# Full-height stationary operands and one address residue for the operand pools of a hybrid attention block

## The chip, the cores and the metric

The kernel runs on one core of one Trainium2 chip. The metric is the device time of one execution in microseconds (us); the time of a version is the median of its runs.

## The reference

One decoder layer on x of 1024 tokens by 1024 features, all in fp32. With h = RMSNorm(x), one projection h @ W_in gives the inputs of three token mixers and their gates:

```
y_A = differential attention, 4 heads: softmax(q0 k0) - lam * softmax(q1 k1), times v of width 128
y_B = sliding window (128) attention with sinks, 8 query heads on 2 kv heads
y_C = compressed + selected + window (512) attention, 8 query heads on 2 kv heads, gated sum of three
x  <- x + W_o( sum_n sigmoid(G_n) * (y_n @ P_n) )
x  <- x + W_down relu(W_up RMSNorm(x))^2
```

A relative position bias is added to the token logits. For the compressed branch, keys and values of 32-token blocks are pressed through a small MLP, which leaves 63 positions (64 with padding) for each of the two kv heads.

## The kernel before, in words

**Products.** Each fp32 product is made of three matmuls (`mm3`, L115 to L120): every operand is split into a high and a low part in the fp32r format (`split`, L87: ScalarE writes the high part, VectorE or GpSimd the low part), and high x high (L118), high x low (L119) and low x high (L120) are summed in PSUM. In the trace a matmul is written `out<-moving,stationary`.

**Stages, in order of time.** (1) Norm and transposition of x (`norm_transpose`), the projection of the first head of A, the bias vectors and the compression MLP; (2) mixer A, head by head, to about 416 us; (3) mixer B; (4) mixer C, for each of its two kv heads a projection (`project_c`) followed by the attention items (`items_c`), from about 572 to 1210 us; (5) the branch products, W_o and the MLP. The MLP's two products use a seven-product (Strassen) form: 16 pairs x 7 products x 12 matmuls of 512 columns each way.

**Order.** TensorE's instructions run in the order in which the program emits them. `mix` (L155) interleaves the attention's steps ("fine") with pieces of dense work (the next projection, or the sigmoid gates of `gates`) by fixed estimates of TensorE and VectorE time. The instructions of the other engines, and the DMA queue of SyncE, are ordered by a planner that simulates the program.

**Mixer A's keys.** `project_a` projects q, k, v of a head, and `vec` writes a tile `tm` for each 128 tokens: q high/low of both components (256 columns), k high twice for each component (L588, 256 columns), k low of both components (L590, 128 columns). `to_state` transposes `tm` in groups of up to four blocks of 128 columns into one PSUM tile `tr` (L552) and copies the group into the state `st` (L556 on ScalarE, L558 on VectorE). The five blocks make a group of four and a group of one. In a logits row (`logits`, L702) there are two matmuls for each of the two components: the first has all 128 rows (q high and q low against k high, written twice), the second 64 rows (q high against k low); `n["logits"]` (L576, L577) holds the slices. For each head, tokens 0 to 511 make 2 such rows for each 128 tokens and tokens 512 to 1023 make 4: 24 a head, 96 in all.

**Mixer C's compressed values.** `compressed` (L1085) writes probabilities `pc` of 128 queries x 64 positions; `tp_c` transposes two of them (64 rows of output), and `pv_c` multiplies with `vct`, the compressed values as 64 rows x 128 columns (high and low side by side): two matmuls (L895, L896) for each of 32 items.

**Where tiles lie.** Pools are stacked from the left and from the right end of each partition's memory; a pool's address is the sum of the sizes before it. The addresses modulo 512 bytes, as the program of before lays them out:

| operand | stage | residue |
|---|---|---|
| `hh`, `hl` (normed x, transposed) | 1 to 4 | 480 |
| state `st` / weight forms `wh`, `wl` | mixers A, B | 320 / 320 + 64 k, k = 0 to 7 |
| state `st`, weight forms `wh`, `wl`, `xh`, `xl` | mixer C | 192 |
| probabilities `ph`, `pl` | mixers A, B / C | 160 / 480 |
| `mh`, `ml` (merged x), `t2` to `t4`, half of the branch weights, second half of `oc` | stage 5 | 416 |
| `ob`, first half of `oc`, `wo`, the other weight forms | stage 5 | 480 |
| `ident`, `identr` | all | 384, 416 |

**Bias vectors.** `bias_vectors(p0)` (L244) loads `rb`, `oh`, `mk`, multiplies (L378), adds into `bv` (L379) and stores to memory. It is emitted behind the first projection, with its tiles in the pool `p0` beside the tiles of x and the gain `g`.

## Time and profile before

| what | us |
|---|---|
| median of 3 runs | 2076.6 (2073.64 to 2076.71) |
| the profiled execution | 2073.64, its span 2073.6 |
| TensorE matmuls busy | 1950.6 (94%) |
| weight loads busy | 1615.6 (78%) |
| VectorE, ScalarE, GpSimd busy | 1420.5, 1019.3, 948.4 |

The span of the profiled execution is its device time to a tenth of a microsecond; nothing lies around it. Matmuls are pipelined: a row's duration is longer than what the matmul costs. The cost is the step from the start of one matmul to the start of the next, and most of the readings below are such steps. PEld is the engine's weight load, which can run while the matmul before it still streams. "issue" as the end of an idle time means that the engine waited for nothing that the profile shows.

### The profile page before, as it was taken

How to read it: one execution, taken by the hardware profiler on the slowest of the kernel's cores; microseconds unless marked ns; L12 is line 12 of the kernel's file. 1: busy time of each engine (PE TensorE's matmuls, PEld its weight loads, DVE VectorE, ACT ScalarE, POOL GpSimd, SP SyncE). 2: the span in 40 equal slices, each digit the busy share in tenths (PEclk: the TensorE clock that was granted, in tenths of full speed). 3: DMA queues.
4: the chain of work that ended last, by engine and by line, in shares of the span. 5: the costliest groups of instructions: out<-in, count | busy, mean ns of one | idle time of the engine just before them, and what ended most of it. 6: DMA issues, size and time to landing. Idle time of an engine off the chain costs nothing. (4 is left out here: it accounts for less than half of the span.)

```text
span 2073.6 us, 30616 instructions
## 1 busy us (share of the span) xinstructions
PE 1950.6 (94%) x9806; PEld 1615.6 (78%) x9806; DVE 1420.5 (69%) x3231; ACT 1019.3 (49%) x2626; POOL 948.4 (46%) x1137
## 2 busy tenths in 40 slices
PE   7999998998899999999999899999899998999998
PEld 7777777788688788787888677787688886888876
DVE  6757677788838767648676745657755444889898
ACT  5456555566636555536555533325445544434331
POOL 4555345354252212152221327217444444789784
PEclk9999999999999999999999899999999999999998
DMA  6131012011201111202142556425544346345343
GB/s 216 50 102 52 3 55 58 14 50 37 85 24 64 54 53 50 71 30 93 61 151 64 168 180 208 153 89 159 173 163 155 138 143 249 121 158 168 122 142 112
DMA packets 122557, 219.47 MB, mean 106 GB/s; under 512 B 14420, under 2 KB 35412, under 8 KB 122396
## 3 DMA queue, kind: packets, MB, share of 16 engines
q1 hardware_dynamic: 120812, 211.75, 31.3%
q10 hardware_dynamic: 1584, 5.77, 0.8%
q8 instruction: 77, 1.26, 0.3%
q14 instruction: 84, 0.69, 0.1%
HBM read 156.59 MB, written 64.81 MB: 107 GB/s over the span
## 5 line engine op out<-in xcount | busy, mean ns | idle before, releaser
L91 POOL TENSOR_TENSOR wl<-wr,wh 128x512 fp32r<-128x512 f32 (+3 forms) x246 | 326.1, 1332 | 282.1 <-ACT wh L90 236.8
L90 ACT ACTIVATE wh<-wr 128x512 fp32r<-128x512 f32 (+3 forms) x258 | 150.4, 591 | 182.3 <-PE mm L119 122.5
L705 PE MATMUL sc<-st 128*128 128x256 f32 (+5 forms) x736 | 201.6, 356 | 15.4 <-ACT p L737 15.0
L90 ACT ACTIVATE ph<-tr 128x384 fp32r<-128x384 f32 (+3 forms) x280 | 138.3, 496 | 118.0 <-PE tr L753 97.1
L91 DVE TENSOR_TENSOR pl<-tr,ph 128x384 fp32r<-128x384 f32 (+3 forms) x280 | 155.3, 558 | 45.7 <-ACT ph L90 42.4
L750 POOL MEMSET ph<- 128x128 f32 x152 | 34.7, 228 | 301.2 <-PE ac L895 256.6
L705 PEld LDWEIGHTS sc<-st 128*128 128x128 f32 x736 | 126.3, 192 | 55.7 <-ACT p L737 23.4
L118 PE MATMUL mm<-hh,wh 128*128 128x512 f32 x384 | 160.0, 417 | 0.0
L120 PE MATMUL mm<-hh,wl 128*128 128x512 f32 x384 | 152.5, 397 | 0.0
L119 PE MATMUL mm<-hl,wh 128*128 128x512 f32 x384 | 152.4, 397 | 0.0
L119 PE MATMUL mm<-wl,wh 128*128 128x512 f32 x352 | 140.4, 399 | 9.4 <-POOL wl L91 9.4
L118 PE MATMUL mm<-wh 128*128 128x512 f32 x352 | 140.5, 399 | 8.3 <-DVE x L1464 5.4
L753 PE MATMUL tr<-ident,p 128*128 128x128 f32 x792 | 132.3, 280 | 15.4 <-ACT o L883 7.9
L90 ACT ACTIVATE wh<-u 128x512 fp32r<-128x512 f32 x162 | 93.1, 620 | 107.8 <-PE mm L119 28.0
L120 PE MATMUL mm<-wh,wl 128*128 128x512 f32 x352 | 139.7, 397 | 0.0
L737 ACT ACTIVATE p<-sc,mc 128x256 f32<-128x256 f32 (+5 forms) x200 | 106.8, 538 | 51.0 <-DVE mc L729 48.9
L895 PE MATMUL ac<-ph,st 128*128 128x256 f32 x392 | 111.4, 302 | 17.2 <-DVE ob L902 11.3
L91 POOL TENSOR_TENSOR wl<-s,wh 128x512 fp32r<-128x512 f32 x64 | 87.8, 1379 | 82.8 <-ACT wh L90 82.8
L118 PE MATMUL mm<-wh,hh 128*128 128x384 f32 (+1 forms) x320 | 124.6, 389 | 0.0
L91 DVE TENSOR_TENSOR wl<-u,wh 128x512 fp32r<-128x512 f32 x98 | 110.4, 1128 | 4.1 <-ACT wh L90 4.1
L896 PE MATMUL ac<-pl,st 128*128 128x256 f32 x392 | 106.6, 293 | 5.8 <-DVE pl L91 5.2
L753 PEld LDWEIGHTS tr<-ident,p 128*128 128x128 f32 x792 | 92.0, 142 | 24.8 <-ACT o L883 10.5
(309 smaller groups left out, 5759.6 us busy)
## 6 DMA issues: line engine op xcount, KB each, us to landing
ud<-u SPq DMA_DIRECT2D x112, 256.0 KB, 2.1
u<-ud SPq DMA_DIRECT2D x98, 256.0 KB, 3.3
wr<-wu SPq DMA_DIRECT2D x76, 256.0 KB, 2.8
wr<-wd SPq DMA_DIRECT2D x64, 256.0 KB, 2.9
gd<-go SPq DMA_DIRECT2D x48, 256.0 KB, 2.0
g<-gd SPq DMA_DIRECT2D x48, 256.0 KB, 3.1
wr<-wg SPq DMA_DIRECT2D x40, 256.0 KB, 2.6
wr<-wbr SPq DMA_DIRECT2D x40, 256.0 KB, 3.0
```

What stands on the lines that cost most here:

```text
L90: nc.scalar.activation(hi, src, AF.Copy)
L91: (eng or nc.vector).tensor_tensor(lo, src, hi.bitcast(F32), op=ALU.subtract)
L118: mm(out, lh, rh, start=first, stop=False, skip_group_check=more)
L119: mm(out, lh, rl, start=False, stop=False, skip_group_check=more)
L120: mm(out, ll, rh, start=False, stop=last, skip_group_check=more)
L705: self.nc.tensor.matmul(ps[:, off:off + k1 - k0], q[:, t * P:(t + 1) * P], k[:, k0:k1], start=i == 0, stop=i == 1)
L737: self.nc.scalar.activation(p, ps, AF.Exp, bias=m, scale=-1.0, accum_out=l)
L750: nc.gpsimd.memset(ph[0:rows, o:o + P].bitcast(F32), 0.0)
L753: nc.tensor.transpose(pt[0:rows, o:o + P], src, self.ident)
L895: nc.tensor.matmul(ac, v, ph, start=first, stop=False)
L896: nc.tensor.matmul(ac, v, pl, start=False, stop=last)
```

## The change

The key's low part is written twice like its high part, so `tm` gets six blocks, the state grows from 7 x 1024 to 8 x 1024 columns, and the second logits matmul has 128 rows: (q high, q low) against (k low, k low). The compressed values get 64 zero rows, and the four `pc` tiles become fixed tiles of 128 columns whose upper half is zero, taken in turn. Spacer tiles of 96, 480 and 224 bytes move the left pools. By the sums of the sizes, the left pools of mixer C and of stage 5 and `ident`, `identr`, `kct`, `vct` come to residue 480, the states of A and B to 96 and their weight forms to 96 + 64 k. The bias vectors' tiles move from `p0` to the next pool `cp`, which takes `p0`'s place, and their sum is written in place.

```
-        self.st_n, self.tm_n = 7 * S, 768
+        self.st_n, self.tm_n = 8 * S, 768
...
-            self.bias_vectors(p0)
         with tc.tile_pool(name="cp", side="right", **kw) as cp:
+            self.bias_vectors(cp)
...
+        self.pcs = [self.at.tile([P, P], F32, name=f"pc{i}") for i in range(4)]
+        for x in self.pcs:
+            nc.gpsimd.memset(x[:, 64:P], 0.0)
...
     def idents(self):
+        self.cst.tile([P, 24], F32, name="gap0")
         self.ident = self.cst.tile([P, P], F32, name="ident")
...
         nc.vector.memset(self.nhalf, -0.5)
+        self.cst.tile([P, 120], F32, name="gap1")
...
+        c.tile([P, 56], F32, name="gap2")
         self.kct = c.tile([P, 2, P], F32R, name="kct")
-        self.vct = c.tile([64, 2, P], F32R, name="vct")
+        self.vct = c.tile([P, 2, P], F32R, name="vct")
+        nc.gpsimd.memset(self.vct[64:P].bitcast(F32), 0.0)
...
-        bv = pool.tile([20, 2, 384], F32, name="bv")
...
-            nc.vector.tensor_tensor(bv[:, i, :], ps[0:20, 0:384], mk[:, i, :], op=ALU.add)
+            nc.vector.tensor_tensor(mk[:, i, :], ps[0:20, 0:384], mk[:, i, :], op=ALU.add)
...
-                self.split(self.vct[:, :, 0:64], self.vct[:, :, 64:128], vr)
+                self.split(self.vct[0:64, :, 0:64], self.vct[0:64, :, 64:128], vr)
...
-        n = dict(st=st, v=st[:, 5 * S:7 * S].rearrange("p (t x e) -> p t x e", x=2, e=P), logits=[])
+        n = dict(st=st, v=st[:, 6 * S:8 * S].rearrange("p (t x e) -> p t x e", x=2, e=P), logits=[])
         for c in range(2):
-            half = slice(64 * c, 64 * c + 64)
-            n["logits"].append([(st[:, c * S:c * S + S], st[:, (2 + c) * S:(3 + c) * S]),
-                                (st[half, c * S:c * S + S], st[half, 4 * S:5 * S])])
+            q = st[:, c * S:c * S + S]
+            n["logits"].append([(q, st[:, (2 + c + x) * S:(3 + c + x) * S]) for x in (0, 2)])
...
-            kl = tm[:, 512:640].rearrange("p (c d) -> p c d", d=HD)
-            nc.vector.tensor_tensor(kl, y[:, 2:4, :], kd[:, :, 0, :].bitcast(F32), op=ALU.subtract)
+            kl = tm[:, 512:768].rearrange("p (c x d) -> p c x d", x=2, d=HD)
+            nc.vector.tensor_tensor(kl, y[:, 2:4, :].unsqueeze(2).to_broadcast([P, 2, 2, HD]), kd.bitcast(F32),
+                                    op=ALU.subtract)
...
-        return self.project(self.a["wa"][h], 384, vec, (st, [i * S for i in range(5)])), n
+        return self.project(self.a["wa"][h], 384, vec, (st, [i * S for i in range(6)])), n
...
-                    return hv(self.vct[:, g, :], ph[0:64, 0:256], pl[0:64, 0:256], True, False)
+                    return hv(self.vct[:, g, :], ph[:, 0:256], pl[:, 0:256], True, False)
...
-        p = mem["c"] = self.at.tile([P, 64], F32, name="pc", tag="pc", bufs=4)
+        p = mem["c"] = self.pcs[0]
+        self.pcs.append(self.pcs.pop(0))
...
-        self.expo(p, ps, m[:, 0, 0:1], l[:, 0, 0:1])
+        self.expo(p[:, 0:64], ps, m[:, 0, 0:1], l[:, 0, 0:1])
```

## The prediction

> **What bounds the kernel now.** I read, in this order, the page's head, the busy time by stretches, the waits, and then the order of time, where the step from one matmul's start to the next is what counts. First the stretches (columns: us, then busy us and count for each engine):

> ```profile
> span 2073.6 us, 30616 instructions
> ...
> 130.00:416.00 286.00, 267.41 (x1460) 216.65 (x1459) 202.99 (x586) 157.12 (x524) 126.78 (x193) 1.00 0.13 38
> 624.00:884.00 260.00, 250.44 (x1428) 211.43 (x1427) 184.99 (x604) 150.29 (x427) 55.37 (x113) 1.00 0.18 57
> 1508.00:1560.00 52.00, 52.00 (x225) 41.89 (x224) 26.42 (x36) 26.05 (x43) 24.22 (x19) 1.00 0.44 152
> 1768.00:1820.00 52.00, 52.00 (x231) 43.05 (x230) 44.55 (x57) 22.34 (x41) 40.04 (x27) 1.00 0.42 135
> ```

> TensorE is the bound in each: 94% in mixer A (130 to 416), 96% in C's first items, all of the time in the MLP's up product (1508) and down product (1768). VectorE, the next, has 71% in A and in C. So what counts is how long TensorE takes over its fixed list, and who would stop it if it went faster. Its waits in A, and one from C, say what it stops for now (us in all, times, longest):

> ```profile
> PEld sc L705 <- issue: 21.0, 85, 0.3
> PEld mm L118 <- issue: 13.7, 62, 0.2
> PEld tr L753 <- ACT o L883: 7.7, 8, 1.1
> PEld tr L753 <- DVE pl L91: 5.2, 5, 1.3
> ...
> PE ac L895 <- DVE ob L902: 4.2, 5, 1.0
> ```

> The two largest are waits for nobody: 34.7 us of "issue" before weight loads. They sit around the 64-row loads:

> ```profile
> 137.66 0.71 PE L705 MATMUL sc<-st 128*128 128x384 f32 x2
> 137.93 0.18 PEld L705 LDWEIGHTS sc<-st 64*128 64x128 f32 x1 [0.25 <-issue]
> 138.30 0.19 PEld L118 LDWEIGHTS mm<-wh,hh 128*128 128x128 f32 x1 [0.19 <-issue]
> 138.30 0.44 PE L118 MATMUL mm<-wh,hh 128*128 128x384 f32 x1
> 138.41 0.19 PEld L119 LDWEIGHTS mm<-wl,hh 128*128 128x128 f32 x1
> 138.58 0.34 PE L119 MATMUL mm<-wl,hh 128*128 128x384 f32 x1
> 138.76 0.34 PE L120 MATMUL mm<-wh,hl 128*128 128x384 f32 x1
> ```

> A full-height load begins while the matmul before it streams (138.41 beneath the one of 138.30). The 64-row load starts only at 137.93, and the full load behind it at 138.30, together with its own matmul. Three matmuls of 384 columns take 138.58 - 137.66 = 0.92 us, where the undisturbed step is 138.76 - 138.58 = 0.18: 0.38 us lost for each logits row.

> **The change part by part.** The sum is made against the profiled execution, 2073.6 us, which is 3.0 below the median of 2076.6.

> *The key's low part in 128 rows.* There are 96 such rows, so TensorE's list shrinks by 96 x 0.38 = 36.5 us (the 34.7 of "issue" is the same thing seen by the loads). The second matmul streams as many columns as before, so I give it the first one's step. Added in each of the 32 token blocks: one more transposition, a ScalarE copy of 256 columns instead of 128 (L556) and a low part of 256 columns instead of 128 (L590):

> ```profile
> L556 ACT ACTIVATE st<-tr 128x128 fp32r<-128x128 f32 x24 | 6.4, 266 | 6.5 <-PE tr L552 6.5
> L556 ACT ACTIVATE st<-tr 128x256 fp32r<-128x256 f32 x4 | 1.5, 381 | 2.7 <-PE tr L552 2.7
> L590 DVE TENSOR_TENSOR tm<-y,tm 128x128 fp32r<-128x128 f32 x24 | 8.7, 362 | 1.5 <-ACT tm L588 1.1
> ```

> The copy grows by 0.115 us (3.7 in all, ScalarE); the low part I let grow as much (3.7, VectorE). A transposition costs TensorE no more than the (794.54 - 794.13) / 4 = 0.10 us of the rows below: 3.3 us in all. The list is then 33 us shorter. How much arrives? VectorE's share of A would rise from 203 / 286 = 71% to 207 / 253 = 82%, and the waits on VectorE and ScalarE around the transpositions (7.7 and 5.2 us among them) will grow: the probabilities (L91) and the copies come later by TensorE's clock. I take 0.7, since TensorE's list, some 250 us, stays well above VectorE's 207: 23 us. Ends: 33 (nothing new waits) and 13.

> *The compressed values in 128 rows.* One of the 32 places, and full-height matmuls of the same shape:

> ```profile
> 793.37 0.40 PE L120 MATMUL mm<-hh,wl 128*128 128x512 f32 x1
> 793.70 0.38 PE L895 MATMUL ac<-ph,vct 64*128 64x256 f32 x1
> 793.92 0.28 PE L896 MATMUL ac<-pl,vct 64*128 64x256 f32 x1
> 794.13 0.66 PE L753 MATMUL tr<-ident,p 128*128 128x128 f32 x4
> 794.54 0.48 PE L118 MATMUL mm<-hh,wh 128*128 128x512 f32 x1
> ...
> 837.81 0.28 PE L895 MATMUL ac<-ph,st 128*128 128x256 f32 x1
> 838.05 0.28 PE L895 MATMUL ac<-ph,st 128*128 128x256 f32 x1
> ```

> From 793.37 to 794.13 are 0.76 us. Undisturbed it would be one step of 512 columns (0.23, below) and two of 0.12 (838.05 - 837.81, two steps): 0.47. So 0.29 x 32 = 9.2 us. The wider `pc` adds nothing: its transpositions stream `ident`, 128 columns as before, and the split of their output works on more partitions, not more columns. The four clears of `pcs` and the one of `vct` go to GpSimd, which is busy 55 of 260 us in C: nothing, and a microsecond at each start if that cover is gone.

> ```profile
> L753 PEld LDWEIGHTS tr<-ident,pc 128*64 128x64 f32 x64 | 6.8, 110 | 2.1 <-DVE pc L1040 2.0
> ```

> These loads of 64 columns show no "issue" at all, only 2.0 us of waiting for VectorE, so making them 128 wide gains nothing. [...]

> *One residue.* Steps of 512 columns differ by place. In the MLP the counts above are of nothing but 512-column matmuls, back to back: 52 / 225 = 231 ns in the up product (moving operands at residue 416, stationary ones at 480) and 52 / 231 = 225 in the down product (all 480); matmuls cut by a window's ends are counted too, so the difference is what to read: 6 ns. C's projection is like the up product (72 steps between the first two rows, 16.80 us: 233 ns), and the branch products give the control, since their weights alternate between two pools within the same loop (12 steps between rows):

> ```profile
> 571.93 0.40 PE L118 MATMUL sc<-wh,hh 128*128 128x512 f32 x1
> 588.73 0.40 PE L118 MATMUL sc<-wh,hh 128*128 128x512 f32 x1
> ...
> 1300.38 0.39 PE L118 MATMUL mm<-oc,wh 128*128 128x512 f32 x1
> 1303.13 0.40 PE L118 MATMUL mm<-oc,wh 128*128 128x512 f32 x1
> 1305.92 0.39 PE L118 MATMUL mm<-oc,wh 128*128 128x512 f32 x1
> ```

> Weights at 416 like the moving operand: 2.75 / 12 = 229 ns; weights at 480: 2.79 / 12 = 233. So I take it that equal residues save 4 to 6 ns a step, and 6 where the whole stage is unequal now. Up: 16 x 7 x 12 = 1344 steps, 8.1 us, all of it on the path, as TensorE never stops there. C's projections: 384 steps, 2.3. The 20 gate features in C: 960 steps, 5.8. W_o and the branches: some 580 steps of 2 ns, 1.0. A and B keep unequal residues (96 + 64 k against 480, one form in eight equal): nothing. Ends: up 6.5 and 9, W_o and branches 0 and 2, the projections 0 and 2.3.

> In C the values and the gates make 9.2 + 5.8 = 15.0 us of a list that hardly waits for others (the 4.2 us above is the largest); I take 0.8 of it, 12, with ends 15 and 7.

> *The bias vectors' tiles in the next pool.* They now lie where `g` and x lay, so their loads wait until the last norm (L135) has read `g`:

> ```profile
> 17.60 5.46 SPq L249 DMA_DIRECT2D w<-w  x7
> 23.17 0.36 SPq L214 DMA_DIRECT2D x<-x  x1
> ...
> L372 SPq DMA_DIRECT2D oh<-c_oh x1: 327/327/327, 16.8 to 16.8; - x1
> DMA to landing us min/median/max: 5.9/5.9/5.9
> L135 DVE SCALAR_TENSOR_TENSOR xn<-x,ss,g x8: 1284/1548/1926, 7.8 to 45.1; 128x1024 f32<-128x1024 f32 x8
> L378 PE MATMUL sc<-oh,rb x4: 481/481/494, 62.0 to 62.9; 32*20 32x384 f32 x4
> ```

> The last norm ends by 47.0, so `oh` lands at about 53.2, 8.8 us before L378 needs it at 62.0. SyncE's queue behind it could stand still meanwhile, but the planner doesn't issue in the program's order: the last load of x, emitted before `w1`, was issued after it. Cost nothing, covered by those 8.8 us; each microsecond beyond them would stop TensorE at L378.

> *Sum:* 23 + 12 + 2.3 + 8.1 + 1.0 = 46.4 us, so 2073.6 - 46.4 = 2027.2; the runs lie up to 3 us above: 2028.

> **The rivals.** (1) *VectorE paces A.* Then A gives some 8 us, not 23, and the time is 2043. For it: 82% of an engine with in-order waits. Against: today's waits of TensorE on others in A are short, the two quoted 1.3 us at most. (2) *Everything arrives*: 33 + 15 + 2.3 + 9 + 2 = 61, 2012. For it: the lost time stands in gaps that wait for nobody. (3) *The residue is a coincidence of stages*: without 4.6 (the gates' share), 2.3, 8.1 and 1.0 it is 2044. Against it stands the control in the branch loop. (4) *The gaps don't come from the 64 rows*, the change doesn't do what it says in A and C: only the residue's 16.0 and the 3.3 of the transpositions are left, 2061. Against: nothing else has a load that waits for "issue". (5) *Slower: a full-height load can't run beneath the matmul before it if that uses the same rows.* Then each of the 160 loads (96 and 64) that get all rows stands on the path with its 0.19 us, +30.4, where the 64-row ones lost less; with +3.3 and -16.0 it gives 2091. It decides once each load shows more than (16.0 - 3.3) / 160 = 0.08 us. Against: the load of 138.41 lies beneath the matmul of 138.30. [...]

> **How the numbers follow.** Forecast 0.62, (1) 0.12, (2) 0.12, (3) 0.06, (4) 0.05, (5) 0.03. The range reaches to (2) below, 2011, and above to the low ends of all terms, 13 + 7 + 0 + 6.5 + 0 = 26.5, 2047, and with a late bias load of a microsecond 2048, which takes in (1) and (3). It leaves out (4) and (5). A change of 0.2% (4 us) is about what can be told from none; only (5) is slower, and a mixture of (4) with a late bias load could end within: faster 0.95, same 0.02, slower 0.03.

> **What would show it.** In the changed kernel's rows: no 64-row form of L705 and L895, no "issue" before L705 and L118 in A, and three steps of 0.18 where 0.92 us stood; 52 us of the up product with about 231 matmuls; A some 23 us shorter, with longer waits of the transpositions on L91 and L883, and VectorE near 80%. The prediction is wrong if A's waits take back more than half, if a stretch of C or the up product keeps its count, or if L378 waits for its loads.

## The result and the profile after

The changed kernel takes 2039.9 us (median of 4 runs, 2039.29 to 2045.69), the kernel before on the same chip 2075.1 (4 runs, 2072.13 to 2076.71). The ratio is 0.9831, 95% interval 0.9813 to 0.985: some 35 us are gone. The forecast was 2028 (2011 to 2048).

The profiled execution of after has a span of 2043.7 us and a device time of 2045.69: 2.0 us lie around the span. So the sentence ahead of the prediction that nothing lies around the span of before (2073.6) is probably wrong, and its profile belonged to an execution of some 2075.6, which is none of the four. That would put the forecast at 2029, which alters nothing below.

The stretches of after that answer to those of before (us, then busy us and count of each engine, granted clock, DMA share, GB/s):

```profile
span 2043.7 us, 30701 instructions
...
131.00:406.00 275.00, 244.12 (x1511) 226.39 (x1511) 208.22 (x591) 163.39 (x532) 131.54 (x201) 0.98 0.15 41
616.00:874.00 258.00, 247.78 (x1437) 213.84 (x1435) 184.05 (x599) 149.83 (x426) 53.72 (x109) 1.00 0.19 61
1484.00:1536.00 52.00, 52.00 (x232) 43.03 (x231) 29.26 (x39) 26.34 (x44) 25.48 (x19) 1.00 0.46 159
1740.00:1792.00 52.00, 52.00 (x231) 43.08 (x230) 44.79 (x57) 21.98 (x41) 40.42 (x28) 1.00 0.42 137
```

TensorE's share of A fell from 94% to 89% (244.12 of 275), VectorE's rose to 76%, and the granted clock in A is 0.98 where it was 1.00. (The prediction had said near 80% for VectorE.) The up product now has the down product's count.

Where the time went in the profiles, each stage taken from its first matmul to the first of the next. "Again" is a second profile of the same changed kernel, from the last experiments:

| stage | before | after | gain | gain, again | forecast |
|---|---|---|---|---|---|
| up to A | 128.2 | 130.1 | -1.9 | -1.7 | 0 |
| A | 291.7 | 276.1 | 15.6 | 17.9 | 23 |
| B, first half | 81.1 | 85.5 | -4.4 | -4.5 | 0 |
| B, second half | 71.0 | 70.1 | 0.9 | -0.3 | 0 |
| C, two projections | 96.8 | 96.0 | 0.8 | 1.6 | 2.3 |
| C, items | 547.8 | 537.4 | 10.4 | 14.2 | 12 |
| branches and W_o | 193.2 | 192.7 | 0.6 | -1.1 | 1.0 |
| up | 326.0 | 319.2 | 6.8 | 6.5 | 8.1 |
| down and end | 337.8 | 336.6 | 1.2 | 1.1 | 0 |
| span | 2073.6 | 2043.7 | 29.9 | 33.7 | 46.4 |

The rows that were to show the change, in the order of time. First a logits row in A:

```profile
306.03 0.34 PE L120 MATMUL mm<-wh,hl 128*128 128x384 f32 x1
306.20 0.51 PE L711 MATMUL sc<-st 128*128 128x384 f32 x2
306.55 0.34 PE L118 MATMUL mm<-wh,hh 128*128 128x384 f32 x1
306.73 0.34 PE L119 MATMUL mm<-wl,hh 128*128 128x384 f32 x1
```

Two logits matmuls and the dense one behind them take 306.73 - 306.20 = 0.53 us, three steps of 0.18, where 0.92 stood. No load in A waits for "issue" any more. The compressed values in C (780.88 to 781.33, 0.45 us where 0.76 stood; forecast 0.47), and the branch loop, where the weights of both pools now lie at the residue of `oc`:

```profile
780.88 0.39 PE L120 MATMUL mm<-hh,wl 128*128 128x512 f32 x1
781.10 0.28 PE L901 MATMUL ac<-ph,vct 128*128 128x256 f32 x1
781.22 0.28 PE L902 MATMUL ac<-pl,vct 128*128 128x256 f32 x1
781.33 0.60 PE L759 MATMUL tr<-ident,p 128*128 128x128 f32 x4
...
1267.37 0.39 PE L118 MATMUL mm<-oc,wh 128*128 128x512 f32 x1
...
1272.81 0.39 PE L118 MATMUL mm<-oc,wh 128*128 128x512 f32 x1
```

The 24 steps between the last two rows take 5.44 us: 227 ns each, where 229 and 233 took turns.

So every edit does at its place what it was said to do. What is missing is lost between those places, some three quarters of it in A and in B's first half. A can be split into three parts: TensorE's waits (its idle gaps over 0.15 us), what half-clock spells add (half of the matmul time that lies in them), and the rest, which is TensorE's own list, in before with the 0.38 us that each of the 96 logits rows lost at its 64-row load (called a drain from here on):

| A, us | before | after | again |
|---|---|---|---|
| list | 273.1 | 240.4 | 240.7 |
| waits | 18.6 | 30.6 | 29.7 |
| half-clock spells | 0 | 5.1 | 3.4 |
| sum | 291.7 | 276.1 | 273.8 |

The list is 32.7 us shorter, which is the 33 of the prediction. Of that the waits take back 12.0 and the spells 5.1. The main waits of TensorE in A (us in all, times, longest), first of before, then of after:

```profile
PE tr L753 <- ACT o L883: 5.8, 8, 0.9
PE tr L753 <- DVE pl L91: 4.1, 5, 1.1
...
PE sc L705 <- ACT p L737: 1.7, 3, 1.1
```

```profile
PE sc L711 <- ACT p L743: 10.2, 13, 2.3
PE tr L759 <- ACT o L889: 5.8, 8, 0.8
PE tr L759 <- DVE pl L91: 4.9, 5, 1.3
```

The two waits that the prediction quoted as going to grow hardly did: the one on L91 went from 4.1 to 4.9, the one on the output's scaling (L889 now) stayed at 5.8. With the copies into the state, the transpositions' waits grew by some 3.4 us in all. Most of the growth is another wait: a logits matmul that waits for the exponentials (L743) of an earlier row, from 1.7 us to 10.2. The logits have three PSUM buffers, so a row takes the buffer of the row three before it, once an exponential has read that one. One such place, TensorE, ScalarE and VectorE in turn:

```profile
306.20 0.51 PE L711 MATMUL sc<-st 128*128 128x384 f32 x2
307.08 0.63 PE L711 MATMUL sc<-st 128*128 128x512 f32 x2
309.87 0.62 PE L711 MATMUL sc<-st 128*128 128x384 f32 x2 [1.63 <-ACT p L743]
```

```profile
309.04 0.69 ACT L743 ACTIVATE p<-sc,m 128x512 f32<-128x512 f32 x1 [0.86 <-DVE m L735]
```

```profile
306.70 0.43 DVE L595 TENSOR_TENSOR tm<-y,tm 128x256 fp32r<-128x256 f32 x1 [0.18 <-ACT tm L593]
307.06 0.28 DVE L727 TENSOR_REDUCE m<-sc 128x1 f32<-128x128 f32 x1
307.26 0.28 DVE L91 TENSOR_TENSOR tm<-y,tm 128x128 fp32r<-128x128 f32 x1
307.46 0.15 DVE L728 TENSOR_TENSOR m<-m 128x1 f32<-128x1 f32 x1
307.53 0.42 DVE L595 TENSOR_TENSOR tm<-y,tm 128x256 fp32r<-128x256 f32 x1
307.86 0.68 DVE L725 TENSOR_REDUCE m<-sc 128x1 f32<-128x512 f32 x1
308.46 0.48 DVE L735 CUSTOM_DVE_ANT_0 sc<-sc,bias,m 128x256 f32<-128x256 f32 x1
```

The row's last logits are written from 306.20 on, its minimum (L735) starts only at 308.46, the exponential behind it at 309.04, and TensorE stands from 308.24 to 309.87. In between VectorE works on the projection's query and key parts (L91, L595), on the row's own first minimum (L727, L728) and on the next row's (L725).

The same place in before shows what had covered this:

```profile
315.06 0.70 PE L705 MATMUL sc<-st 128*128 128x384 f32 x2
...
318.13 0.81 PE L705 MATMUL sc<-st 128*128 128x384 f32 x2 [0.28 <-ACT p L737]
```

There the minimum starts at 316.68, so minimum and exponential take 1.45 us until the buffer is taken again, and in after they take 309.87 - 308.46 = 1.41. But between the logits that the minimum needs last (315.06 in before, 306.20 in after) and the matmul that takes the buffer, TensorE's own matmuls took 2.79 us and now take 2.03: two rows without their drains of 0.38. I matched the twelve such waits of after behind the first one with the same rows of before: TensorE's own work between is 0.5 to 0.8 us shorter at every one, and from the minimum's start to the exponential's end it is 1.2 to 1.3 us in after (1.2 to 1.8 in before). So the drains had covered the logits' own chain. That is read from the rows; no experiment lengthens the cover alone.

The second loss shows in the granted clock. The same times in after and in before:

```profile
413.70:417.10 3.40, 3.40 (x15) 3.29 (x14) 2.03 (x7) 1.29 (x5) 1.19 (x3) 0.50 0.33 103
```

```profile
413.70:417.10 3.40, 2.82 (x19) 2.62 (x19) 2.47 (x6) 2.67 (x9) 3.40 (x7) 1.00 0.21 60
```

In after TensorE has half the clock for 3.4 us. Between 100 and 540 us there are five such spells in after (at 137, 267, 345, 414 and 461), three of them in A, and none in before. The number differs from profile to profile: in A it is two in the second profile of the change, and one in two kernels whose keys are as before (p3_residue and s2_before_first below). In a spell a step takes 0.32 us instead of 0.18:

```profile
137.72 0.52 PE L119 MATMUL mm<-wl,hh 128*128 128x384 f32 x1
138.04 0.52 PE L120 MATMUL mm<-wh,hl 128*128 128x384 f32 x1
```

The last loss is at the start of B, where a product with the values waits once for the values' low part on GpSimd, a wait that before does not have. It stands partly in the place of another, on VectorE. First before, then after:

```profile
PE ac L895 <- DVE ob L902: 4.6, 4, 2.0
```

```profile
PE ac L901 <- DVE ob L908: 3.2, 3, 2.0
PE ac L901 <- POOL st L91: 2.4, 1, 2.4
```

TensorE's waits in B's first half are 9.7 us before and 11.0 after, so 1.3 of the 4.4 us lost there are waits; the two spells at 414 and 461 add 3.4.

### The profile page after: what moved, and what is told of

Its sections match the earlier page's. It is cut to its first block, busy times and chain, and to the rows that moved or that the text cites. A ratio compares the mean times of both kernels' runs of the same rounds, so it can differ in the third digit from the quotient of the medians.

```text
span 2043.7 us, 30701 instructions
## 1 busy us (share of the span) xinstructions
PE 1901.7 (93%) x9838; PEld 1621.5 (79%) x9838; DVE 1423.4 (70%) x3231; ACT 1022.0 (50%) x2626; POOL 954.3 (47%) x1142
## 5 line engine op out<-in xcount | busy, mean ns | idle before, releaser
L91 POOL TENSOR_TENSOR wl<-wr,wh 128x512 fp32r<-128x512 f32 (+3 forms) x246 | 328.8, 1343 | 275.0 <-ACT wh L90 238.8
L90 ACT ACTIVATE wh<-wr 128x512 fp32r<-128x512 f32 (+3 forms) x258 | 150.3, 590 | 183.8 <-PE mm L119 124.1
L711 PE MATMUL sc<-st 128*128 128x256 f32 (+5 forms) x736 | 183.9, 344 | 25.9 <-ACT p L743 25.3
L90 ACT ACTIVATE ph<-tr 128x384 fp32r<-128x384 f32 (+3 forms) x280 | 138.4, 497 | 105.5 <-PE tr L759 87.0
L91 DVE TENSOR_TENSOR pl<-tr,ph 128x384 fp32r<-128x384 f32 (+3 forms) x280 | 155.8, 559 | 40.2 <-ACT ph L90 37.6
L711 PEld LDWEIGHTS sc<-st 128*128 128x128 f32 x736 | 122.8, 192 | 47.5 <-ACT p L743 38.8
L118 PE MATMUL mm<-hh,wh 128*128 128x512 f32 x384 | 158.8, 414 | 0.0
L120 PE MATMUL mm<-hh,wl 128*128 128x512 f32 x384 | 151.5, 395 | 0.0
L119 PE MATMUL mm<-hl,wh 128*128 128x512 f32 x384 | 151.4, 394 | 0.0
L119 PE MATMUL mm<-wl,wh 128*128 128x512 f32 x352 | 139.5, 396 | 9.4 <-POOL wl L91 9.4
L118 PE MATMUL mm<-wh 128*128 128x512 f32 x352 | 139.9, 398 | 8.2 <-DVE x L1471 5.3
L90 ACT ACTIVATE wh<-u 128x512 fp32r<-128x512 f32 x162 | 93.0, 620 | 106.3 <-PE mm L119 27.9
L120 PE MATMUL mm<-wh,wl 128*128 128x512 f32 x352 | 139.1, 395 | 0.0
L743 ACT ACTIVATE p<-sc,mc 128x256 f32<-128x256 f32 (+5 forms) x200 | 106.7, 538 | 52.0 <-DVE mc L735 47.0
L91 POOL TENSOR_TENSOR wl<-s,wh 128x512 fp32r<-128x512 f32 x64 | 89.5, 1405 | 79.3 <-ACT wh L90 79.3
L118 PE MATMUL mm<-wh,hh 128*128 128x384 f32 (+1 forms) x320 | 117.0, 366 | 0.0
L91 DVE TENSOR_TENSOR wl<-u,wh 128x512 fp32r<-128x512 f32 x98 | 112.5, 1150 | 3.9 <-ACT wh L90 3.9
L902 PE MATMUL ac<-pl,st 128*128 128x256 f32 x392 | 106.5, 292 | 6.5 <-DVE pl L91 5.8
L91 POOL TENSOR_TENSOR wl<-u,wh 128x512 fp32r<-128x512 f32 x64 | 98.8, 1557 | 25.1 <-ACT wh L90 25.0
```

Of the source, the lines that this page charges most:

```text
L90: nc.scalar.activation(hi, src, AF.Copy)
L91: (eng or nc.vector).tensor_tensor(lo, src, hi.bitcast(F32), op=ALU.subtract)
L118: mm(out, lh, rh, start=first, stop=False, skip_group_check=more)
L119: mm(out, lh, rl, start=False, stop=False, skip_group_check=more)
L120: mm(out, ll, rh, start=False, stop=last, skip_group_check=more)
L711: self.nc.tensor.matmul(ps[:, off:off + k1 - k0], q[:, t * P:(t + 1) * P], k[:, k0:k1], start=i == 0, stop=i == 1)
```

## The experiments

The first four ran on one chip (before: 2072.3, median of 11 runs). The first three are each one part of the change.

**p1_keys**, the keys alone:

```
-                                (st[half, c * S:c * S + S], st[half, 4 * S:5 * S])])
+            n["logits"].append([(q, st[:, (2 + c + x) * S:(3 + c + x) * S]) for x in (0, 2)])
...  (six blocks, 8 x 1024 columns of state, the bias vectors' tiles in cp)
```

> The kernel before with the key's low part in 128 rows alone (state of 8 x 1024 columns, bias vectors in the next pool). Theory T1 (the list of TensorE gets 33 us shorter in A, and waits for the exponentials and the copies take back about half): 15 to 22 us faster, nothing changed outside A. Rival T2 (the drains were hidden behind other waits, the whole gain of the change lies in the residues and the values): within 4 us of before. Rival T3 (everything arrives, what was missing in the changed kernel was lost elsewhere): 30 us or more.

Measured: 2057.4 us, ratio 0.9926 (0.9913 to 0.9939), 14.8 us faster, just short of the 15 to 22 expected. In its profile A is 17.3 us shorter and B's first half 4.3 longer, which was not expected. **p2_values**, the compressed values alone:

```
-        self.vct = c.tile([64, 2, P], F32R, name="vct")
+        self.vct = c.tile([P, 2, P], F32R, name="vct")
-                    return hv(self.vct[:, g, :], ph[0:64, 0:256], pl[0:64, 0:256], True, False)
+                    return hv(self.vct[:, g, :], ph[:, 0:256], pl[:, 0:256], True, False)
```

> The kernel before with the compressed values and pc in 128 rows alone. T1: 32 places of 0.29 us in C, four fifths of them on the path: 6 to 9 us faster. T2': VectorE paces C, nothing: within 3 us.

Measured: 2066.0, ratio 0.9964 (0.995 to 0.9977), 6.3 us faster. **p3_residue**, the three spacers alone:

```
+        self.cst.tile([P, 24], F32, name="gap0")
+        self.cst.tile([P, 120], F32, name="gap1")
+        c.tile([P, 56], F32, name="gap2")
```

> The kernel before with the three spacer tiles alone: no instruction differs but by addresses. T1 (equal residues modulo 512 save 4 to 6 ns for each matmul of 512 columns in C's projections and gates, the branches, W_o and the up product): 10 to 15 us faster, 7 to 8 of it in the up product. Rival (the stage, not the residue, makes the step): within 3 us, up product unchanged.

Measured: 2058.9, ratio 0.9938 (0.9924 to 0.9953), 13.4 us faster; the up product gains 6.4, where 7 to 8 were expected. That product, and the same stretch with the keys alone:

```profile
1494.00:1546.00 52.00, 52.00 (x231) 43.07 (x230) 26.99 (x36) 26.66 (x46) 26.87 (x20) 1.00 0.50 171
```

```profile
1500.00:1552.00 52.00, 52.00 (x225) 41.89 (x224) 26.29 (x36) 27.80 (x46) 24.53 (x19) 1.00 0.42 147
```

231 against 225 matmuls: the spacers do it, and nothing else of the change. The whole stage goes from 326.0 to 319.7 us. Together the three parts are worth 14.8 + 6.3 + 13.4 = 34.5 us, the whole change 35.3: within the noise they add, and none hides another. The keys are the part that falls short: 14.8 of a list that is 33 us shorter. They alone bring the waits: TensorE's waits in A are 30.1 us with p1_keys, 17.8 and 18.9 with the other two parts.

**p4_shared**: the whole change, but the second logits matmul goes with all its 128 query rows against the one low block of before, which holds the low parts of both components' keys. So the sixth block, its transposition, the wider copy and the wider subtraction are not there, nor the larger state and the move of the bias vectors. The product of the query's low part is then with the other component's key low part.

```
-            n["logits"].append([(q, st[:, (2 + c + x) * S:(3 + c + x) * S]) for x in (0, 2)])
+            n["logits"].append([(q, st[:, (2 + c) * S:(3 + c) * S]), (q, st[:, 4 * S:5 * S])])
```

> The changed kernel with five blocks as before: the second logits matmul takes all 128 rows of q (high and low) against the block of k low of both components, as it is, not written twice. What it adds to the high x low product is q low of one component times k low of the other instead of its own, a term of the size of those that the three-product form leaves out anyway. No sixth transposition, no wider copies, no larger state, bias vectors where they were. If these additions were part of what A lost: 4 to 9 us faster than the changed kernel (2031 to 2036). If they were covered: within 2 us of it.

Measured: 2029.3, ratio 0.9798 (0.978 to 0.9815). On another chip (before: 2073.7, 17 runs) it stood beside the change itself. **s0_change**, the changed kernel, and **s3_shared**, this one again:

> The changed kernel itself, on one chip with the shared-low-block kernel. Theory 'what is added in the 32 token blocks (a transposition, half a copy, half a subtraction) costs TensorE 3.3 us and the rest is paid in waits': 5 to 9 us slower than the shared low block (0.983 against 0.980). Theory 'the difference of the earlier call was its chip': within 2 us of it.

> The shared-low-block kernel again: 0.978 to 0.982 of before, as in the first call.

Measured: 2042.4, ratio 0.9842 (0.9824 to 0.986), and 2031.9, ratio 0.9796 (0.9781 to 0.9812). The intervals don't meet: what the change adds in each token block, with the bias move, costs 0.0046 x 2073.7 = 9.5 us, just above the 5 to 9 expected and, by the intervals, somewhere between 5 and 14. Between these two profiles lie 1.8 us before A, 5.8 in A and 2.5 in B's first half. Not all of the 5.8 is the added work: A takes 272.8 us in p4_shared's profile and 268.0 in s3_shared's, which is the same kernel, for spells and waits that fall otherwise; the list without them is 238.8 and 239.2, against 240.7. The wait for GpSimd at B's start stands with the same 2.4 us in all three profiles of kernels with six blocks (the change twice, p1_keys) and in none with five. In A the logits' waits are smaller, but far from 1.7:

```profile
PE sc L711 <- ACT p L743: 10.6, 13, 2.6
```

```profile
PE sc L711 <- ACT p L743: 8.6, 12, 2.4
```

So a small part of what A gave back belongs to the added work, and 8 us of waits remain without it. The next four ask what paces the exponentials, all built on the shared block and run on one chip (before: 2072.3, 11 runs).

**r1_act**, one ScalarE instruction instead of two:

```
-            for c in range(2):
-                nc.scalar.activation(kd[:, c], y[:, 2 + c:3 + c, :].to_broadcast([P, 2, HD]), AF.Copy)
+            nc.scalar.activation(kd, y[:, 2:4, :].unsqueeze(2).to_broadcast([P, 2, 2, HD]), AF.Copy)
```

> The kernel with the shared low block (ratio 0.9798, 2029 us), and in it the doubling of the key's high part, two ScalarE instructions in each of 32 token blocks, is one instruction of the same 256 columns. Theory 'ScalarE's queue paces the exponentials that free the logits' PSUM buffers': ScalarE has some 32 x 0.3 = 10 us less in mixer A, the waits of the logits for the exponential fall by 3 us or more, and the time is 2 to 5 us below the shared-low-block kernel (ratio about 0.978). Theory 'VectorE's minimum comes late, and the exponential only waits for it': within 1.5 us of it (0.979 to 0.9805). Theory 'the spacing of other work between the rows': within 1.5 us too.

**r2_pool**, the low part on GpSimd:

```
-            nc.vector.tensor_tensor(kl, y[:, 2:4, :], kd[:, :, 0, :].bitcast(F32), op=ALU.subtract)
+            nc.gpsimd.tensor_tensor(kl, y[:, 2:4, :], kd[:, :, 0, :].bitcast(F32), op=ALU.subtract)
```

> The kernel with the shared low block, and in it the key's low part (a subtraction of 128 columns in each of 32 token blocks, 0.36 us each on VectorE) is done by GpSimd: VectorE has 11.6 us less in mixer A. Theory 'VectorE's queue is what the exponentials wait for': the logits' waits for their PSUM buffer fall by 3 us or more, and the time is 2 to 5 us below the shared-low-block kernel (ratio about 0.978). Theory 'ScalarE paces': within 1.5 us. [...]

Measured: r1_act 2032.0, ratio 0.9806 (0.9784 to 0.9829); r2_pool 2037.2, ratio 0.983 (0.9806 to 0.9853). Neither is faster than 0.9798 (r2_pool is slower, if anything), and the logits' waits in A did not fall (first r1_act, then r2_pool):

```profile
PE sc L710 <- ACT p L742: 9.8, 12, 2.8
```

```profile
PE sc L711 <- ACT p L743: 8.2, 13, 2.2
```

But neither edit took off the load that it was to take. In r1_act one instruction of 0.41 us replaces two of 0.30, and ScalarE's busy time in A falls by only some 2 us (162 to 160.4) instead of 10. In r2_pool other instructions of VectorE grew longer (L835 over 1024 columns from 1.52 to 1.87 us), and its busy time falls by 3.5 us (206 to 202.7) instead of 11.6; the subtraction took 0.53 us on GpSimd. So the two runs show that 2 and 3.5 us less on these engines moved no wait, and don't rule out that a load paces.

**r3_slow** and **r4_fast**, the spacing of the dense work:

```
-PACE = (1.6, 1.4144, 1.156, 1.392, 1.45, 1.7)
+PACE = (1.8, 1.4144, 1.156, 1.392, 1.45, 1.7)      (r4_fast: 1.4)
```

> The kernel with the shared low block, and the factor by which the planner of mixer A spaces its dense work (the projections' pieces) between the rows is 1.8 instead of 1.6, everything else the same. Theory 'the spacing, set when the rows were longer, is off now': one of this run and the one with 1.4 is 2 to 5 us faster than 1.6, the other slower by as much. Theory 'an engine's queue paces, not the spacing': both within 2 us of 1.6, or both slower.

> As the run before with the factor at 1.4. Theory 'spacing': faster by 2 to 5 us if 1.8 is slower, slower if 1.8 is faster. Theory 'an engine's queue paces': within 2 us, or slower like 1.8.

Measured: 2047.2, ratio 0.9878 (0.9857 to 0.99), and 2047.9, ratio 0.9888 (0.9868 to 0.9909). Against the shared block (0.9798) they lose 17 and 19 us, most of it in A (286 and 288 us long, against 273), where I had expected 2 to 5. With 1.8 it is the clock, 0.95 over A, and about as much the waits, 38.0 us in all against 29.0 in p4_shared, 14.8 of them for the exponentials; with 1.4 it is nearly all waits, 42.8 us, 24.8 of them for the exponentials. First the stretch and the wait with 1.8, then the wait with 1.4:

```profile
129.00:414.00 285.00, 246.89 (x1485) 230.11 (x1485) 203.19 (x591) 162.94 (x538) 135.21 (x207) 0.95 0.15 44
```

```profile
PE sc L711 <- ACT p L743: 14.8, 9, 2.8
```

```profile
PE sc L711 <- ACT p L743: 24.8, 17, 3.7
```

The spacing of the matmuls moves these waits far more than the two edits before did. But 1.6 is the best of the three, so a spacing that the shorter rows had put far off is not the explanation; values between were not tried.

**s1_first** gives the minimum and the exponentials of A priority on VectorE and ScalarE, and **s2_before_first** does the same in the kernel before. TensorE's list is the same in s1_first, instruction by instruction.

```
+                with self.tc.high_priority(offset=self.urgent):
                     ... (far_min, near_min, and the two calls of expo in items_a)
```

> The shared-low-block kernel with VectorE's row minimum and ScalarE's exponentials of mixer A given the priority that the splits of the probabilities have; TensorE's order stays the same, instruction by instruction, only VectorE's and ScalarE's order changes. Theory 'the minimum stands behind the projection's work in VectorE's queue, and that holds the logits' PSUM buffers': the logits' waits for the exponential fall from 8 us to under 4 and the time by 2 to 6 us (ratio 0.977 to 0.979). Theory 'whatever VectorE does first, something else is late by as much': the logits' waits fall, those of the transpositions grow, and the time stays within 2 us or rises. Theory 'the exponential is late for another reason': nothing moves.

> The kernel before with that same priority. There the logits hardly wait for the exponentials (1.7 us), so by the first theory there is nothing to gain: within 3 us of before, or slower by what the transpositions then wait. If it gains as much as the run with the shared block does, the queue's order was a cost already before the change, and not one that the change brought out.

Measured: s1_first 2027.5 us, ratio 0.9781 (0.9761 to 0.98); s2_before_first 2073.9, ratio 1.0001 (0.9989 to 1.0014). The first looks like a hit, and isn't. The logits' waits in A are what they were with the shared block (8.6):

```profile
PE sc L711 <- ACT p L743: 8.1, 12, 2.1
```

A takes 269.0 us against 268.0. At the place that the change's profile showed above, the minimum now starts 1.14 us behind the row's logits instead of 1.61 (2.26 in the change), but the exponential finds ScalarE at the copies of the projection (L521, L90) and the wait falls only from 0.97 to 0.67: the chain still takes 2.68 us, and TensorE's own work between 2.01. The 6.7 us between the two profiles lie mainly in B (1.9) and in C's second half (5.0). There VectorE's and ScalarE's order is the same in both kernels, and the stage differs by 3.4 us between profiles of the other kernels with the shared block too (274.9 to 278.3, here 273.3). Its interval overlaps that of s3_shared, so an edge over it isn't shown. The theory of the queue's order fell in this form.

What stays open is what would make the 8 us go: a shorter chain of logits, minimum, exponential and buffer, or more of TensorE's work within it. The order on VectorE and ScalarE was tried, their load only by a little, and a fourth buffer for the logits, which would put a further row into the cover, was not. Of the 10.2 us, 2.3 are one wait at A's first rows, where the minimum stands for the DMA of the bias; before has 1.1 there.

## Why the prediction was right, and where its sum was off

The time lies inside the range, 12 us above the forecast. By the number alone it is nearer to rivals (1) and (3), 2043 and 2044, than to the 2028; it is the stages and the parts that tell them apart. Step by step:

*The 64-row drains.* Right: 0.38 us for each of 96 rows, three steps of 0.18 afterwards, no "issue" left. The rivals that denied it, (4) and (5), are out. The loads of the row of 306.20, all full-height and some 0.18 us each, lie beneath the matmuls before them (the two of L711 from 306.03 to 306.39, that of L118 from 306.38), and the steps stay at 0.18.

*How much of the keys arrives.* This is the term that was mis-sized: 23 us, measured 14.8 alone, inside the forecast's own ends (33 and 13) but near the lower. The list was right: 33 us shorter by the forecast, 32.7 by the trace. The factor of 0.7, which no row measured, allowed 10 us for what comes back; in A 17.1 came back, and 4.4 more in B's first half:
- TensorE's waits in A grew by 12.0 us, 8.5 of them the logits' own, for a PSUM buffer. The prediction looked at who waits now and let those waits grow; the one that had nearly nothing (1.7) grew instead. The drains had been part of what hid it.
- The half-clock spells, three in A (5.1 us) and two in B's first half (3.4), were not in the sum at all. How many there are is in part chance: the second profile has two in A.
- The added work was priced at 3.3 us of TensorE and nothing elsewhere. With the bias move it costs 9.5, part of it in the two items above, and a wait of 2.4 at B's start, on GpSimd, which the prediction did not name for this step.

Rival (1), VectorE paces A, was to leave 8 us of the 23. The 14.8 lie halfway between, so the number doesn't decide, and r2_pool took too little off VectorE to do so. The waits that end on VectorE in A grew by some 3 us and those on ScalarE by 9; at the two longest waits but the first, 1.7 and 1.6 us, the minimum also stood behind other work of VectorE. In-order waits of VectorE can be seen in before: it stood 0.69 us, to 143.27, for the logits of a minimum (L719), though the input of the subtraction behind it (L590, from 143.61) had been written by 142.45. So VectorE has a share, and the rival as it was put isn't shown. Rival (2), everything arrives, is out. By its own sign the prediction was close to wrong: A's waits were not to take back more than half, and they took 12.0 of 32.7 us, with the spells 17.1.

*The values and the gates in C.* Forecast 12, measured 10.4 and 14.2 in two profiles. Both parts are seen alone in C's items: 8.7 us with p2_values, where the places lose 9.2, and 6.6 with p3_residue, where 5.8 were forecast.

*The residue.* Forecast 8.1 in the up product, measured 6.8, 6.5 and 6.4 (p3_residue); the counts of 231 and 232 came out. The step was, if anything, priced too low: between neighbouring 512-column matmuls at full clock it falls from 233.3 to 226.8 ns on the mean, which is 8.6 us over the 1325 such steps. (The 229 of the control in the branch loop was a mixture: single steps there are 226 and 227, or 231 and 236 in turn.) What failed is "TensorE never stops there". In the up product it stops twice, each time for a sum (`u`) on VectorE, and the stops are longer now. The longer of the two, before and after (the other went from 1.2 to 1.5 us):

```profile
PE mm L118 <- DVE u L1381: 7.8, 1, 7.8
```

```profile
PE mm L118 <- DVE u L1388: 8.9, 1, 8.9
```

So 1.5 us of the 8.6 went into these waits; the rest of the difference is small and lies mostly in half-clock spells. Rival (3), a coincidence of stages, is out: the branch loop's two residues became one step of 227 ns, and p3_residue, 13.4 us faster, has the spacers alone.

*The wider `pc`, W_o and the branches:* nothing and a microsecond, within what two profiles differ by. The transpositions of `pc` take 273 ns on the mean where 274 stood, and the split of their output 382 ns on ScalarE and 421 on VectorE over 128 partitions, where 374 and 412 stood over 64.

*The bias vectors' late load.* Right that it is covered. `oh` was issued at 47.41, its product started at 63.7 and waited for no load:

```profile
47.41 0.31 SPq L379 DMA_DIRECT2D oh<-c_oh x1
```

```profile
L384 PE MATMUL sc<-oh,rb x4: 481/481/495, 63.7 to 64.7; 32*20 32x384 f32 x4
```

That product starts 1.7 us later than before, behind a half-clock spell at 38 us which both profiles of the change have and no other kernel has, p1_keys with its moved load included. What brings it about isn't shown.

## What to carry to other kernels

Where a stationary operand of fewer rows stands between full ones, look at the step from start to start around it: here 0.38 us were lost each time in A and 0.31 at the place shown in C, and filling the rows was worth it even where the filling was multiplied for nothing (6.3 us with p2_values). Fill them with what is already there: the block that held both low parts did the doubled copy's work, but for a small term, and was some 9.5 us cheaper. When time is taken out of the bound engine's list, ask what that time had covered: for each buffer that the engine takes, those with hardly any wait today too, how much of its own work hides the chain that frees it. Then ask how close the waits that remain lie: here 168 of 170 stretches of 3.41 us with 1.9 us and more of idle time were followed by a spell at half the clock.

## What the runs showed of the hardware that was not expected

| idle in a stretch of 3.41 us | followed by a spell | not |
|---|---|---|
| under 1.33 | 0 | 7607 |
| 1.33 to 1.7 | 19 | 117 |
| 1.7 to 1.9 | 34 | 33 |
| 1.9 and more | 168 | 2 |

The ends of matmuls are modelled, so the bounds are not sharp. The longest single gap ahead of the five spells in A and B of after is 2.4 us, and two of them (267, 414) follow stretches in which no gap is over 1.0 us but the sum is 1.8. In these two it is the sum that goes with the spell, not the longest gap; over all profiles 168 of the 170 stretches with 1.9 of 3.41 us idle, in pieces too, were followed by one. Runs of one kernel differ in the granted clock too: the profiled run of after has a mean of 0.980 and is 6 us above the other three (0.982 to 0.984).

*The residue.* The up product's matmuls of 512 columns, at full clock, take 226 to 227 ns from start to start where moving and stationary operands have the same address modulo 512 bytes. Where the addresses differ, its steps are mostly 231 and 236 in turn, 233 on the mean. C's projections go from a mean of 234 to 228 with equal residues and the branch loop from 230 to 227, and the up product changes with the three spacers as the only edit. That the modulus is 512, and that equal residues are what counts, is the author's reading of the layout; no run tries another distance.
